# Per-token gate matrices by accumulating scatters in place of TensorE products, with 160 tokens instead of 128 on the gathered path

## The chip, the cores and the metric

One Trainium2 chip, one core. The metric is the device time of one execution in microseconds (us). Five engines work side by side: TensorE (PE, with its weight loads PEld), VectorE (DVE), ScalarE (ACT), GpSimd (POOL) and SyncE (SP), and 16 DMA engines, to which SP, ACT and POOL issue transfers.

## The reference

The kernel is one layer of a decoder on 512 prompt tokens and 8 sample tokens (520 in all, model width 2048, float32). The change touches the second half, a retrieval over 16384 experts, each of which is one row of `u` and one row of `v`:

```python
def peer_route(hn, wq, subkeys):
    q = (hn @ wq).reshape(t, PEER_HEADS, 2, PEER_DKEY // 2)
    s = jnp.einsum('thcd,cnd->thcn', q, subkeys)
    half_s, half_i = lax.top_k(s, PEER_TOPK)
    ...
    experts = (i1 * PEER_NKEYS + i2).reshape(t, -1)
    return experts, jax.nn.softmax(best_s, axis=-1).reshape(t, -1)

def one_chunk(args):
    xc, ec, gc = args
    act = jax.nn.gelu(jnp.einsum('cd,ced->ce', xc, u[ec]))
    return jnp.einsum('ce,ced->cd', gc * act, v[ec])
```

Here `hn` is the normed output of the attention half. Each token picks 8 heads x 16 = 128 expert numbers `ec` with gates `gc`, and its output is the sum over them of gate x gelu(hn . u[e]) x v[e]. An expert number that two heads of a token pick counts twice.

## The kernel before

**Two paths for the tokens.** The first `ND` = 392 tokens are computed densely against all experts: expert tile i is 128 rows of `u`; `u_tile` (line 925) multiplies it by the 392 tokens (16 chunks of the model width, three products each, since each float32 operand is split into a high and a low part: 48 products of 128x392), scales by the norm on DVE (line 930) and applies gelu on ACT. The activation is multiplied by a gate matrix (line 1218; mostly zeros, one number per token and expert), split again (lines 1220 and 1221) into `C`, and multiplied with tile i of `v` in `v_group` (line 1238), which sums over `GRP` = 4 tiles in PSUM and adds the sum to `acc` on DVE (line 1263). The other `NS` = 128 tokens take the gathered path (`gathered`, line 1139): for each of a token's 128 picks POOL gathers 128 rows of 8 KB (one per token, line 1155) from `u`, DVE multiplies and sums them (line 1185); then the same with `v` (line 1197).

**Gate matrices.** After the routing, `build_g` (line 1068) makes, per 4 tokens, one-hot matrices on DVE (lines 1097, 1099), weights them with the gates on ACT and POOL (lines 1101 to 1104), and PE multiplies them (line 1080: 8 products of 128x128), one 128x128 gate matrix per token. ACT copies them to `stg`, and POOL stores 14 pieces to the DRAM tensor `g_d`, from which `load_g` fetches the part of 4 expert tiles.

**Order.** The order of PE and SP is written by hand; POOL's too, from the gathered path on. The other engines are ordered by a scheduler. PE's work is the clock: each 16 products of 260 columns (or as many columns) make one tick (`TICK`), and side work is cut into steps, one of which is emitted per tick. While routing and `build_g` run as such steps, PE computes `u` tiles ahead of their gates: `spill_u` (line 938) stores 70 activations (`NSPILL`) to `act_d`, and `c_of` fetches them later. From `start_experts` (line 1126) on, `v` groups alternate with the `u` tiles that were not spilled, and a gathered row is taken up each `PACE` = 3.1 ticks.

**Weights.** SP loads each weight tile (1 MB) into `wr` (two buffers); ACT rounds it to the high part `wh`, DVE subtracts to the low part `wl`, in halves (lines 297, 299).

**Before the routing.** The `wout` products (line 883) give `acc` for 520 tokens in two products of 260 columns. The operands `HH`, `HG` (high) and `HL`, `HLG` (low) of the dense and the gathered tokens are made from `acc` without the norm; the norm's sum of squares is finished after the first query product (`q_product(0)`, line 911), and the norm multiplies the results (lines 1116, 930).

Of the kernel before, what the change touches and what calls it, by code (L numbers as in the profile page):

```python
# [45 lines left out]
ND, NS = 392, 128  # L46
TT, NTT = 128, 5
TILES = [(ND, NS)] + [(i * (ND // 4), ND // 4) for i in range(4)]
GC, NGC = 28, 14
KA = 12  # L50
NEXP = 128
NSPILL = 70
GRP = 4
TICK = 16
NACT = 3
COPY_EVERY = 9
# [3 lines left out]
NCB = 6  # L60
NGB = 3
PACE = 3.1
PRE = 2
LEAD = 3

C_ID, C_IO, C_N1, C_N2, C_QK, C_SK, C_SR, C_MK, C_END = 0, 128, 256, 272, 288, 292, 300, 301, 317
# [25 lines left out]
def _layout(a):  # L92
# [12 lines left out]
    o["v"] = f["peer_v"][0].reshape(NEXP // GRP, GRP, P, 4, 2, 256).transpose(0, 3, 2, 4, 1, 5)  # L105
# [26 lines left out]
    cst[:64, C_MK:C_MK + 16] = np.arange(64)[:, None] // 4 == np.arange(16)  # L132
    o["cst"] = cst
# [18 lines left out]
def _plan():  # L152
# [10 lines left out]
    p += [("uT", i) for i in range(NSPILL)]  # L163
    for g in range(NEXP // GRP):
        p += [("uT", i) for i in range(g * GRP + (g > 0), min(NEXP, g * GRP + GRP + 1)) if i >= NSPILL]
        p += [("v", (g, q)) for q in range(4)]
# [3 lines left out]
def _program(tc, I, O):  # L170
# [16 lines left out]
    onesR = cp.tile([P, P], F32R, name="onesR")  # L187
    V.tensor_copy(onesR, ones)
# [5 lines left out]
    eg = cp.tile([P, 2, P], F32, name="eg")  # L194
# [3 lines left out]

    def halves(dt):
        a, b = slot("S1a", dt, 8), slot("S1b", dt, 8)  # L200
        return lambda k: (a if k < 8 else b)[:, k % 8]

    def parts(dt):
        a, b = slot("S0", dt, KA), slot("S0g", dt, KC - KA)
        return lambda k: a[:, k] if k < KA else b[:, k - KA]
# [21 lines left out]
    g_d = dp.tile([NGC, P, NK, GC], F32, name="g_d")  # L227


    clock = {"n": 0}  # L230
    first, active, queue = deque(), deque(), deque()

    def soon(f, lag=1):
        first.append((clock["n"] + lag, f))

# [11 lines left out]
    def tick():  # L247
        clock["n"] += 1
        if clock["n"] % COPY_EVERY == 0:
            emit_copy()  # L250
        if first and first[0][0] <= clock["n"]:
            first.popleft()[1]()
        else:
            step()

    def drain(all_=True):
        while first:
            first.popleft()[1]()
        while all_ and (active or queue):
            step()  # L260
# [161 lines left out]
    qk = sp = tab = sbias = qs = kn = vn = None  # L422
# [3 lines left out]
    def start_attention():  # L426
        nonlocal qk, sp, tab, sbias, qs, kn, vn
# [3 lines left out]
        sp = at.enter_context(tc.tile_pool(name="sp", bufs=1))  # L431
        tab = sp.tile([P, 512], F32, name="tab")
# [382 lines left out]
    oa = (lambda k: sl["OA"][:, k], lambda k: sl["OA"][:, 8 + k])  # L815
# [21 lines left out]
    for n in range(2):  # L837
        for c in range(KC):
# [6 lines left out]
            if "sample" in sl and "OA" not in sl and not active and not queue and not first:  # L845
                at.close()
                slp = perm.enter_context(tc.tile_pool(name="sl", bufs=1))
                sl["OA"] = slp.tile([P, KC, T], F32R, name="S2", tag="S2")
# [25 lines left out]
    acc = slp.tile([P, KC, T], F32, name="acc", tag="S2")  # L874
    HHt = slp.tile([P, KC, ND], F32R, name="HH", tag="S3")
    HGt = slp.tile([P, KC, NS], F32R, name="HG", tag="S3g")
    ssq = bt.tile([P, T], F32, name="ssq")
    for c in range(KC):
        w = stream(("wout", c))
        if c < 4:  # L880
            S_.dma_start(acc[:, c * 4:c * 4 + 4, :], I["xT"][:, c * 4:c * 4 + 4, :])
        ps = psum_mm()
        dot3(ps, w, (mH, mL))
        V.tensor_tensor(v2(acc[:, c]), v2(acc[:, c]), ps[:, :, :TH], op=OP.add)
        w2 = cst[:, C_N2 + c:C_N2 + c + 1]
        A.activation(HHt[:, c], acc[:, c, :ND], AF.Copy, scale=w2)
        A.activation(HGt[:, c], acc[:, c, ND:], AF.Copy, scale=w2)
        if c == 0:
            A.activation(ssq, acc[:, c], AF.Square)
        else:  # L890
            s = tmp0()
            A.activation(s, acc[:, c], AF.Square)
            V.tensor_tensor(ssq, ssq, s, op=OP.add)
# [3 lines left out]
    hg = (whole(HGt), whole(HLGt))  # L897
    for c in range(KC):
        w2 = cst[:, C_N2 + c:C_N2 + c + 1]
        V.scalar_tensor_tensor(HLt[:, c], acc[:, c, :ND], w2, HHt[:, c], op0=OP.mult, op1=OP.subtract)  # L900
        V.scalar_tensor_tensor(HLGt[:, c], acc[:, c, ND:], w2, HGt[:, c], op0=OP.mult, op1=OP.subtract)


    def q_product(h):
        w = stream(("wq", h))
        ps = psum_mm()
        terms([(ps[:, 0, :ND], 0, ND), (ps[:, 1, :NS], ND, T)],
              [pick(w, k * P) + tuple((d(k), g(k)) for d, g in zip(hw, hg)) for k in range(KC)])
        return ps

    psq = q_product(0)
    psr = psum_mm()
    rms(ssq, [psr[:, h, :TH] for h in range(2)])
    br.close()
    pr = ExitStack()
    rt = ExitStack()
    ix = rt.enter_context(tc.tile_pool(name="ix", bufs=1))
    tk = ExitStack()
    i1T = ix.tile([P, ND], BF16, name="i1T")
    i2T = ix.tile([P, ND], BF16, name="i2T")  # L920
    gH = ix.tile([P, ND], F32R, name="gH")
    gL = ix.tile([P, ND], F32R, name="gL")
    rstd_ = rstd.rearrange("p h t -> p (h t)")

    def u_tile(i):
# [10 lines left out]
    cell = {}  # L936

    def spill_u():
        nonlocal nu
        act = u_tile(nu)  # L940
        G_.dma_start(act_d[nu], act)
# [384 lines left out]
```

## Time and profile before

| | |
|---|---|
| runs (3) | median 3893.84 us, 3890.56 to 3897.88 |
| profiled execution | 3891.22 us, span from first to last instruction 3889.5 us |
| mean granted TensorE clock | 0.993 of full speed |
| PE busy | 3812.2 us, 98% |
| PEld / DVE / ACT / POOL busy | 97% / 71% / 37% / 24% |
| chain that ended last | PE 84%, DVE 8%, DMA 2% |
| DMA | 901.37 MB, mean 232 GB/s |

Share of busy time is read beside the stage: the table of stretches in the rows below gives it by stage. By the timeline, attention and its projections run to about 1170 us, the output products to 1395, queries and routing to 1832, the gate products to 2180, and the alternation of `u` and `v` tiles to the end, with gathered rows from 2257 to 3750.

### The profile page before, as it was taken

What the parts mean: (1) busy time and instruction counts of PE and PEld (TensorE: products, weight loads), DVE (VectorE), ACT (ScalarE), POOL (GpSimd) and SP (SyncE); (2) the same over time, 40 slices, a digit from 0 to 9 for tenths busy, and PEclk for the clock granted to TensorE, in tenths of its full rate; (3) what the DMA queues carried; (4) which work ended last, traced back from release to release, by engine and by line L of the source; (5) the groups of instructions that cost most, each with busy time, mean ns of one, the idle gap of its engine ahead of it and who ended that gap; (6) DMA issues with size and microseconds to landing.
All of it is one profiled execution on the core that took longest, in us unless ns stands there. A gap on an engine that the chain in (4) does not pass through costs nothing.

```text
span 3889.5 us, 61269 instructions
## 1 busy us (share of the span) xinstructions
PE 3812.2 (98%) x25080; PEld 3779.9 (97%) x25080; DVE 2753.0 (71%) x3925; ACT 1436.4 (37%) x2032; POOL 930.5 (24%) x944
## 2 busy tenths in 40 slices
PE   8999999999999999989999999999999999999999
PEld 8999999999999999989999999999999999999999
DVE  5444333778654357898666579999988888888864
ACT  5655444222322322323777532222222323232232
POOL 2111111223210000133666322222222222222200
PEclk9999999999999999999999999999999999999999
DMA  4233334667656333545544579898888889888853
GB/s 164 103 113 137 141 133 183 222 242 260 228 202 236 141 132 116 191 162 197 199 187 184 201 297 336 319 332 318 333 329 330 318 329 337 331 312 304 331 209 131
DMA packets 140761, 901.37 MB, mean 232 GB/s; under 512 B 20096, under 2 KB 21088, under 8 KB 56512
## 3 DMA queue, kind: packets, MB, share of 16 engines
q1 hardware_dynamic: 59296, 489.74, 33.5%
q0 software_dynamic: 66064, 380.27, 26.4%
q10 hardware_dynamic: 15120, 27.43, 2.2%
q8 instruction: 198, 3.24, 0.3%
q14 instruction: 83, 0.68, 0.1%
HBM read 836.48 MB, written 150.95 MB: 254 GB/s over the span
## 4 chain that ended last, share of the span: by engine, by line
PE 84%; DVE 8%; issue 4%; DMA 2%; ACT 1%; POOL 0%; ACTq 0%; POOLq 0%; DVEq 0%
PE mm L336 71%; PE vv L336 8%; DVE wl L299 3%; PE gq L1080 2%; DVE gb L1185 1%; DMA k<-q_d 1%; PE sc L976 0%; ACT wh L297 0%; DMA wr<-in_win 0%; PE a L510 0%; DVE acc L1263 0%; PE a L517 0%; DVE s1b L1048 0%; PE a L523 0%; DVE c L1221 0%
## 5 line engine op out<-in xcount | busy, mean ns | idle before, releaser
L297 ACT ACTIVATE wh<-wr 128x1024 fp32r<-128x1024 f32 x744 | 787.4, 1059 | 1840.3 <-PE mm L336 1454.3
L299 DVE TENSOR_TENSOR wl<-wr,wh 128x1024 fp32r<-128x1024 f32 x744 | 948.3, 1279 | 335.8 <-ACT wh L297 334.0
L336 PE MATMUL mm<-HH,wl 128*128 128x392 f32 x2176 | 755.1, 347 | 15.3 <-DVE wl L299 15.3
L336 PE MATMUL mm<-HH,wh 128*128 128x392 f32 x2176 | 759.1, 349 | 2.1 <-ACT wh L297 1.2
L336 PE MATMUL mm<-HL,wh 128*128 128x392 f32 x2176 | 756.0, 347 | 0.0
L336 PE MATMUL mm<-c,wh 128*128 128x392 f32 x2316 | 608.5, 343 | 3.9 <-DVE c L1221 3.9
L336 PE MATMUL mm<-S,wh 128*128 128x260 f32 x3048 | 589.0, 285 | 8.2 <-ACT S L380 8.2
L336 PE MATMUL mm<-S,wl 128*128 128x260 f32 x2664 | 545.0, 286 | 5.3 <-DVE wl L299 5.3
L336 PEld LDWEIGHTS mm<-S,wh 128*128 128x128 f32 x3048 | 460.2, 190 | 10.4 <-ACT S L380 8.2
L336 PEld LDWEIGHTS mm<-c,wh 128*128 128x128 f32 x2316 | 426.1, 189 | 6.9 <-DVE c L1221 6.1
L336 PEld LDWEIGHTS mm<-HH,wl 128*128 128x128 f32 x2176 | 412.2, 189 | 19.3 <-DVE wl L299 18.6
L336 PEld LDWEIGHTS mm<-S,wl 128*128 128x128 f32 x2664 | 414.5, 190 | 8.8 <-DVE wl L299 5.7
L336 PEld LDWEIGHTS mm<-HH,wh 128*128 128x128 f32 x2176 | 411.5, 189 | 4.0 <-ACT wh L297 1.5
L336 PEld LDWEIGHTS mm<-HL,wh 128*128 128x128 f32 x2176 | 411.6, 189 | 0.9
L336 PE MATMUL mm<-c,wl 128*128 128x392 f32 x1158 | 396.0, 342 | 1.4 <-DVE wl L299 1.4
L336 PE MATMUL mm<-S1a,wh 128*128 128x260 f32 x1520 | 311.0, 286 | 4.2 <-DVE S1a L381 4.1
L336 PE MATMUL mm<-S1b,wh 128*128 128x260 f32 x1520 | 312.2, 287 | 2.1 <-DVE S1b L381 2.1
L336 PE MATMUL vv<-c,wh 128*128 128x392 f32 x1108 | 293.0, 344 | 8.7 <-DVE c L1221 5.5
L1197 DVE SCALAR_TENSOR_TENSOR hb<-gb,dots,hb 128x2048 f32<-128x2048 f32 x127 | 298.1, 2347 | 4.4 <-DMA gb<-in_vn,idx 4.3
L1185 DVE SCALAR_TENSOR_TENSOR gb<-gb,hb 128x2048 f32<-128x2048 f32 x128 | 292.6, 2286 | 3.1 <-DMA gb<-in_un,idx 3.1
L1155 POOL DMA_INDIRECT gb<-in_vn,idx x128 | 158.7, 1240 | 462.5 <-DVE hb L1197 397.3
L336 PEld LDWEIGHTS mm<-S1a,wh 128*128 128x128 f32 x1520 | 235.0, 189 | 6.2 <-DVE S1a L381 5.1
(317 smaller groups left out, 5584.8 us busy)
## 6 DMA issues: line engine op xcount, KB each, us to landing
wr<-in_uT SPq DMA_DIRECT2D x128, 1024.0 KB, 4.9
wr<-in_v SPq DMA_DIRECT2D x128, 1024.0 KB, 7.3
wr<-in_win SPq DMA_DIRECT2D x78, 1024.0 KB, 4.8
g_d<-stg POOLq DMA_DIRECT2D x14, 1792.0 KB, 6.9
ga<-g_d POOLq DMA_DIRECT2D x32, 784.0 KB, 10.8
wr<-in_wout SPq DMA_DIRECT2D x16, 1024.0 KB, 4.8
out_s<-in_c SPq DMA_DIRECT2D x16, 1020.0 KB, 7.3
act_d<-t POOLq DMA_DIRECT2D x70, 196.0 KB, 2.6
```

The source lines that it names most:

```text
L297: A.activation(h, r, AF.Copy)
L299: V.tensor_tensor(l, r, h, op=OP.subtract)
L336: PE.matmul(ps, u, y[lo >= ND][:, lo % ND:hi - lo + lo % ND] if isinstance(y, tuple) else y[:, lo:hi], start=(begin and i == 0 and a == 0) ...
L1080: PE.matmul(ps[:, t], Bt[:, t], AA[:, t, x], start=x == 0, stop=x == 1)
L1155: G_.indirect_dma_start(out=g, out_offset=None, in_=src, in_offset=bass.IndirectOffsetOnAxis(ap=idx[:, j:j + 1], axis=0))
L1185: V.scalar_tensor_tensor(g, g, 1.0, hn, op0=OP.mult, op1=OP.mult, accum_out=dots[:, j:j + 1])
L1197: V.scalar_tensor_tensor(sums, g, coef[:, j:j + 1], sums, op0=OP.mult, op1=OP.add)
```

## The change

1. 360 tokens are dense, 160 gathered (128 in one pass, 32 in another, whose 128 picks are spread over the 128 partitions as 4 x 32). Products of `u` and `v` tiles have 360 columns. The `wout` products are cut into 360 + 160 columns, the query products too.
2. `build_g` is gone. The gate matrices lie in three DRAM tensors (120 tokens each), which SP fills with zeros during the `wout` products (24 stores); POOL then adds the gates with indirect DMAs that accumulate, one for each of the 128 picks of each third: 384, of up to 120 numbers of 4 bytes. Each waits until the one before it on the same tensor has landed.
3. `v` groups sum over 8 tiles instead of 4; one load is one part of 256 columns for 8 tiles.
4. The norm is multiplied into the operands before they are split, so the multiplication at line 930 goes, and the queries wait for the norm. Two query products run chunk by chunk side by side.
5. The spilled tiles are those not in `INLINE`: the set leaves 101 of 128. In each `v` group the remaining one or two `u` tiles stand among the `C` tiles.
6. Gathered rows start after the first routed tile, one each 6.0 ticks during routing, 3.0 during the scatters, 2.6 afterwards. Cache copies are issued each 7 ticks instead of 9.

```diff
-ND, NS = 392, 128
+ND, NS = 360, 160
+NA_, NB_, RB = 128, 32, 4
...
-GRP = 4
+GRP = 8
+GL = 4
+INLINE = {g * GRP + i for g in range(NEXP // GRP) for i in ((0, 4) if g > 4 else (0,))}
+SPILLED = [i for i in range(NEXP) if i not in INLINE]
+NSPILL = len(SPILLED)
...
-COPY_EVERY = 9
+COPY_EVERY = 7
...
-PACE = 3.1
+PACES = {'routing': 6.0, 'gates': 3.0, 'u': 2.6, 'v': 2.6}
+LEAD = 4
+SCATTER = 0.55
...
+        if cell.get("chains"):
+            cell["chains"]()
+        while posts and posts[0][0] <= clock["n"]:
+            posts.popleft()[1]()
+        if pace and clock["n"] >= pace["due"]:
+            pace["due"] += next(pace["gen"], 1e9)
...
+    def blank(t, i):
+        n = NK * P * GC // 8
+        S_.dma_start(g_d[t][i * n:(i + 1) * n].rearrange("(p x n) o -> p x (n o)", p=P, n=GC * 4),
+                     zero.unsqueeze(1).to_broadcast([P, n // P // (GC * 4), GC * 4]))
...
-        dot3(ps, w, (mH, mL))
...
+        dot3(cut2(ps), w, (mH, mL))
...
+    rms(ssq, [psr[:, h, :TH] for h in range(2)])
...
+            V.scalar_tensor_tensor(x[:, lo:hi], a[:, c], w2, rstd_[:, lo:hi], op0=OP.mult, op1=OP.mult)
+            A.activation(h[:, c], x[:, lo:hi], AF.Copy)
+            V.tensor_tensor(l[:, c], x[:, lo:hi], h[:, c], op=OP.subtract)
...
-        pre = tp.tile([P, ND], F32, name="t0", bufs=2)
-        V.tensor_tensor(pre, ps, rstd_[:, :ND], op=OP.mult)
         act = tp.tile([P, ND], F32, name="t1", bufs=2)
-        A.activation(act, pre, AF.Gelu)
+        A.activation(act, ps, AF.Gelu)
...
+        n, act = nu, u_tile(SPILLED[nu])
+        post(lambda: G_.dma_start(act_d[n], act))
...
-                    PE.matmul(ps[:, t], Bt[:, t], AA[:, t, x], start=x == 0, stop=x == 1)
...
+    def scatter():
+        for c in chains:
+            k, s, due = c
+            if s < P and clock["n"] >= due:
+                G_.indirect_dma_start(out=g_d[k], out_offset=bass.IndirectOffsetOnAxis(ap=at_[k][:GC, s:s + 1], axis=0),
+                                      in_=gt_[k][:GC, s:s + 1], in_offset=None, compute_op=OP.add)
+                c[1:] = s + 1, due + 1 / SCATTER
+        return len(chains) == NGC and all(c[1] == P for c in chains)
...
+    while nu < NSPILL:
+        spill_u()
+        if cell.get("stage") == "gates" and scatter():
+            begin()
```

POOL's order while the gates are made. In the program before, during `build_g` (line 941 stores a spilled activation, 1101 and 1104 weight the one-hot matrices, 1088 stores a piece of the gates):

```order
L941 DMA act_d<-t_22203 128x392
L1101 TENSOR_TENSOR AA<-eA,gH 128x128
L1104 TENSOR_TENSOR AA<-eA,gL 128x4x128
L1088 DMA g_d<-stg 128x3584
L1101 TENSOR_TENSOR AA<-eA,gH 128x128
L1104 TENSOR_TENSOR AA<-eA,gL 128x4x128
L941 DMA act_d<-t_22329 128x392
```

In the changed program, during the scatters (line 1126 a scatter into the tensor named, 1192 a gather of rows, 983 the store of an activation):

```order
L983 DMA act_d<-t_20253 128x360
L1126 DMA g_d_94<-gt_15300,at_15297 1966080x1
L1126 DMA g_d_96<-gt_15302,at_15299 1966080x1
L1126 DMA g_d_95<-gt_15301,at_15298 1966080x1
L1192 DMA rowS3g<-in_un,idx 128x2048
L1126 DMA g_d_94<-gt_15300,at_15297 1966080x1
L1126 DMA g_d_96<-gt_15302,at_15299 1966080x1
L1126 DMA g_d_95<-gt_15301,at_15298 1966080x1
L983 DMA act_d<-t_20326 128x360
```

Between two stores, that is for one `u` tile, stand now six to eight scatters and one or two gathers, where POOL had arithmetic. From the first to the last scatter the order holds 384 scatters, 82 gathers, 65 stores of activations, and six pieces of routing arithmetic.

PE's order where the output products end and the queries begin. Before, the sum of squares (line 364) comes after the 96 products of the first query:

```order
L336 MATMUL mm<-HH,wl 128x392
L336 MATMUL mm<-HG,wl 128x128
L364 MATMUL mm<-ssq,ones 128x260 x2
L336 MATMUL mm<-HH,wh 128x392
L336 MATMUL mm<-HG,wh 128x128
```

In the changed program it stands between the last `wout` product and the first of the queries:

```order
L356 MATMUL mm<-S0g,wl 128x360
L356 MATMUL mm<-S0g,wl 128x160
L384 MATMUL mm<-ssq,ones 128x260 x2
L356 MATMUL mm<-HH,wh 128x360
L356 MATMUL mm<-HG,wh 128x160
L356 MATMUL mm<-HL,wh 128x360
L356 MATMUL mm<-HLG,wh 128x160
```

So every query product is now behind the norm, and each pair of products is 360 + 160 columns wide.

## Rows read from the trace of the kernel before

**Rows 1.** Stretches: busy us of each engine (instructions), clock, DMA share, GB/s.

```profile
1832.00:2180.00 348.00, 348.00 (x2244) 347.96 (x2243) 229.28 (x288) 257.13 (x479) 226.70 (x236) 1.00 0.51 190
2290.00:2900.00 610.00, 587.37 (x3214) 579.41 (x3214) 553.26 (x589) 175.00 (x200) 163.75 (x174) 0.99 0.89 329
3200.00:3300.00 100.00, 100.00 (x561) 99.72 (x560) 89.03 (x72) 30.34 (x36) 26.49 (x20) 1.00 0.91 336
```

**Rows 2.** Chain of waits, in order of time: start us, us, what.

```profile
975.14 411.76 PE mm L336 x3432
...
2927.14 42.94 PE mm L336 x240
```

**Rows 3.** Timeline of PE: start us, us, instruction; query products, then gate products.

```profile
1404.19 0.39 PE L336 MATMUL mm<-HH,wh 128*128 128x392 f32 x1
...
1404.48 0.39 PE L336 MATMUL mm<-HL,wh 128*128 128x392 f32 x1
...
1900.86 1.00 PE L1080 MATMUL gq<-AA,Bt 128*128 128x128 f32 x8
1901.70 0.40 PE L336 MATMUL mm<-HH,wl 128*128 128x392 f32 x1
```

**Rows 4.** Timeline at the norm: PE, DVE and ACT, with [idle before <-releaser].

```profile
1396.00 0.47 PE L336 MATMUL mm<-HLG,wh 128*128 128x128 f32 x1 [5.77 <-DVE HLG L901]
...
1386.92 8.15 DVE L900 SCALAR_TENSOR_TENSOR HL<-acc,cst,HH 128x392 fp32r<-128x392 f32 x15 [0.73 <-PE mm L336]
...
1395.60 4.02 DVE L901 SCALAR_TENSOR_TENSOR HLG<-acc,cst,HG 128x128 fp32r<-128x128 f32 x15
...
1413.16 0.84 ACT L366 ACTIVATE rstd<-mm,epst 128x260 f32<-128x260 f32 x2 [5.76 <-PE mm L364]
1414.02 1.28 ACT L367 ACT_TABLE_LOAD   x1
1415.31 0.64 ACT L367 ACTIVATE rstd<-rstd 128x520 f32<-128x520 f32 x1
```

**Rows 5.** Timeline of POOL at the first gathered rows.

```profile
2260.42 0.93 POOL L1155 DMA_INDIRECT gb<-in_un,idx  x1 [0.30 <-issue]
...
2266.82 1.74 POOL L1232 DMA_DIRECT2D t<-act_d  x3
```

**Rows 6.** DMA issues (KB each, median us to landing); the gathers' least, median, most.

```profile
act_d<-t POOLq DMA_DIRECT2D x70, 196.0 KB, 2.6
t<-act_d POOLq DMA_DIRECT2D x70, 196.0 KB, 7.6
st_d<-st POOLq DMA_DIRECT2D x8, 4.0 KB, 6.9
...
DMA to landing us min/median/max: 5.2/8.0/14.8
```

**Rows 7.** Groups by line: busy us, mean ns, idle before.

```profile
L297 ACT ACTIVATE wh<-wr 128x1024 fp32r<-128x1024 f32 x744 | 787.4, 1059 | 1840.3 <-PE mm L336 1454.3 <-PE vv L336 207.5 <-DMA wr<-in_v 29.2
L299 DVE TENSOR_TENSOR wl<-wr,wh 128x1024 fp32r<-128x1024 f32 x744 | 948.3, 1279 | 335.8 <-ACT wh L297 334.0
L1185 DVE SCALAR_TENSOR_TENSOR gb<-gb,hb 128x2048 f32<-128x2048 f32 x128 | 292.6, 2286 | 3.1 <-DMA gb<-in_un,idx 3.1
L1221 DVE TENSOR_TENSOR c<-t,c 128x392 fp32r<-128x392 f32 x107 | 59.4, 563 | 11.0 <-ACT c L1220 10.6
L1263 DVE TENSOR_TENSOR acc<-acc,mm 128x784 f32<-128x784 f32 x171 | 165.9, 970 | 87.4 <-PE mm L336 86.6
L1045 POOL TENSOR_TENSOR s1a<-s1a,s1b 98x2048 f32<-98x2048 f32 (+1 forms) x10 | 50.3, 5028 | 40.9 <-DVE s1a L1043 40.9
```

**Rows 8.** DMA rate in 40 slices of the stretch 2290 to 2900 us.

```profile
GB/s 385 320 340 369 315 346 241 367 369 317 320 211 365 342 348 359 318 366 284 341 318 352 333 223 362 300 363 360 312 337 332 312 300 358 360 353 297 301 392 266
```

More of the change, by code (lines that the diff above doesn't have):

```diff
@@ L226, in _program @@
     act_d = dp.tile([NSPILL, P, ND], F32, name="act_d")
-    g_d = dp.tile([NGC, P, NK, GC], F32, name="g_d")
+    h_d = dp.tile([P, KC, NS], F32, name="h_d")
+    hn_d = dp.tile([NB_, D], F32, name="hn_d")
+    g_d = [dp.tile([NK * P * GC, 1], F32, name=f"g_d{t}") for t in range(NGC)]
     clock = {"n": 0}
+    cell = {}
+    pace = {}
     first, active, queue = deque(), deque(), deque()
@@ L256, in drain @@
     def drain(all_=True):
[L257 to L260, printed above, removed]
+        while first or posts or all_ and (active or queue):
+            if first or posts:
+                (first or posts).popleft()[1]()
+            else:
+                step()
     copies = []
@@ L431, in start_attention @@
         sp = at.enter_context(tc.tile_pool(name="sp", bufs=1))
+        onesR = sp.tile([P, P], F32R, name="onesR")
+        V.tensor_copy(onesR, ones)
         tab = sp.tile([P, 512], F32, name="tab")
@@ L917, in _program @@
     ix = rt.enter_context(tc.tile_pool(name="ix", bufs=1))
+    at_ = [ix.tile([P, P], I32, name=f"at{t}") for t in range(NGC)]
+    gt_ = [ix.tile([P, P], F32, name=f"gt{t}") for t in range(NGC)]
+    chains = []
     tk = ExitStack()
[L919 to L923, printed above, removed]
     def u_tile(i):
@@ L993, in best_all @@
     def best_all():
[L994 removed]
+        s1a = cp.tile([TT, 3072], F32, name="s1a", tag="S1a")
+        s1x = cp.tile([TT, 1024], F32, name="s1x", tag="S1x")
         bs = k1.tile([TT, PH, TOPK], F32, name="bs")
@@ L1053, in best_all @@
                 V.tensor_copy(eg[:, 1], rows[:, 2])
+                cell["stage"] = "routing"
+                perm.enter_context(tc.manual_schedule(engines={mybir.EngineType.PE, mybir.EngineType.SP, mybir.EngineType.Pool}))
+                pace.update(gen=gathered(), due=clock["n"] + 2)
                 yield
                 continue
-            ps = sc_p.tile([P, 512], F32, name="sc")
-            for x in range(3):
-                PE.transpose(ps[:, x * P:x * P + m], rows[:, x], ident[:m, :m])
@@ L1283, in _program @@
         start_experts()
-    perm.enter_context(tc.manual_schedule(engines={mybir.EngineType.PE, mybir.EngineType.SP, mybir.EngineType.Pool}))
-    queue.append(gathered())
+        load_g(0)
+        load_g(1)
+        cell["stage"] = "experts"
+    while nu < NSPILL:
+        spill_u()
+        if cell.get("stage") == "gates" and scatter():
+            begin()
+    if cell.get("stage") != "experts":
+        drain()
+        while not scatter():
+            clock["n"] += 1
+        begin()
+    drain(False)
     c_of(0)
@@ L1290, in _program @@
         if g == NGRP - 1:
-            cell["rush"] = True
-            drain()
+            for _ in pace["gen"]:
+                pass
         v_group(g)
```

381 lines of the change are left out of this document (182 added, 199 removed).

## The prediction, made before the changed kernel was timed

> **What bounds the kernel now.** I read the page first: PE is busy 98% of the span and carries 84% of the chain that ended last, so a product that goes is time, unless another engine steps in. I then went by stretches [rows 1], because the average hides three regimes. While the gate products are made (1832 to 2180 us) PE is busy without a gap, DVE two thirds of the time and DMA half: only PE matters there. From 2290 to 2900 us, when gathered rows run beside `v` groups of spilled tiles, PE is idle for 610 − 587.4 = 22.6 us, DVE is at 91% and DMA at 0.89: all three are near their end. From 3200 us on PE is full again at a DMA share of 0.91. The chain in order of time gives what a product costs in a long run without waits [rows 2]: 3432 of 260 columns in 411.76 us, 120.0 ns each; 240 of 392 columns in 42.94 us, 178.9 ns each. The slope is 58.9 / 132 = 0.446 ns per column, so a product of 360 columns should take 178.9 − 32 x 0.446 = 164.6 ns.
>
> **PE's part of the change.** The dense products of 392 columns become products of 360: 128 `u` tiles x 48 and 16 `v` groups x 16 x 24, 12288 in all, x 14.3 ns = **−175 us**. The gate products go: by the timeline eight of them hold PE for 0.84 us, from 1900.86 to the next product at 1901.70 [rows 3], and there are 98 such groups: **−82 us**; nothing else waited there [rows 1], so all of it is path.
>
> Against that stand narrow products. In the query products a pair of 392 + 128 columns takes 1404.48 − 1404.19 = 0.29 us [rows 3]: 0.179 for the wide one and 0.11 for the narrow one, where the slope alone would give 0.06. The eight gate products, 128 columns too, took 0.105 each. So a product does not come faster than each 0.11 us, and one of 160 columns (0.075 by the slope) will cost 0.11 as well. The `wout` products, 768 pairs of 260 + 260 at 0.240, become 360 + 160 at 0.165 + 0.11 = 0.275: +26 us. The 384 query pairs go from 0.29 to 0.275: −6. Twenty more transposes at 0.11: +2. Together **+22 us**.
>
> **The norm before the queries.** Now PE waits 5.8 us there for the last low operand [rows 4]. After the change the first query product waits for the addition, the squares and their sum (about 1.6 us at the rows' widths), the norm's own product (some 1.1), then logarithm, table load and exponential on ACT (0.84 + 1.28 + 0.64 [rows 4]). By the order DVE then does eight multiplications before the first subtraction: four of 360 at 0.5 and four of 160 at 0.3 (8.15 / 15 and 4.02 / 15 [rows 4], by width), 3.2 us, and 0.5 for the low operand: near 9.5 us. After that DVE makes a chunk in 4 instructions, 1.6 us, for 6 pairs = 1.65 us on PE; the `wl` halves in between cost a further 3 to 4. So 13 in place of 5.8: **+8 us**; ends 0 and +15.
>
> **POOL in the scatter stage: the open price.** No scatter is in the trace. Its nearest rows are the indirect gather, which POOL begins 0.30 us after the one before and holds for 0.93: 1.23 us a step [rows 5]; and, from below, the plain transfer, three in 1.74, 0.57 a step. I take 1.23, since it is the same instruction with as many indices. From the first to the last scatter POOL's order then holds (384 + 82) x 1.23 + 65 x 0.57 + 4 x 5.0 [rows 7] + some 4 = 634 us, beside 65 `u` tiles of 48 x 164.6 ns = 7.9 us, 514 us. POOL would be the bound, by 120 us. PE is coupled to it: gelu needs one of two buffers that POOL's store frees. The buffers and the six spilled tiles after the last scatter give back about 22, so the floor is some +100. At 0.57 a step it would be 381 us, and nothing.
>
> To that come waits. A scatter waits for the one before it on its tensor. Small stores landed in 2.6 us [rows 6], less than the 3.7 that three scatters take, so alone they would not wait. But a transfer that POOL issues behind a gathered row lands behind it: the reloads of activations took 7.6 us, their stores, before the rows began, 2.6 [rows 6]. So in each of the 82 gather intervals (6.3 us of PE) the fourth scatter waits until the row and the first scatter have landed. At the least landing of a gather, 5.2 [rows 6], plus 0.5, it starts at 5.7; with it, 0.7 of another scatter, the store and arithmetic (1.23 + 0.85 + 0.45 + 0.3) the interval takes 8.53 us: 82 x 2.26 = 185 in all, 163 after the slack. I take the middle of 100 and 163: **+132 us**.
>
> The Trainium skill (DMA: Bandwidth & Descriptors, Anatomy of one DMA) puts a fixed cost of about 2.0 us on each DMA that GpSimd issues and calls transfers under 64 KB mostly overhead, which speaks against 384 transfers of 480 bytes. By that figure a scatter has landed before its successor's turn, and only the floor would stand, an estimate of 3781; the rows have small stores at 2.6, and 6.9 for a store of 4 KB [rows 6], so I go by the rows.
>
> **The alternation of `u` and `v`.** For one weight tile (8.6 us of PE) DVE had in the crowded stretch two `wl` halves, 1.46 rows, two additions of 784 and two `C` steps [rows 7]: 2.56 + 3.34 + 1.94 + 1.13 = 9.0 us by durations that overlap a little. After the change, with 10 tiles for 8 experts (7.9 us each), it has 2.56 + 1.6 x 2.29 + 0.8 x 0.89 + 0.8 x 1.04 = 7.8 us: 0.98 of PE's time against 1.04. So I leave the 22.6 us of waits as they are. DMA grows: 10 tiles and 16 rows of 1.05 MB, and 2.6 MB of activations and gates, 29.8 MB in 79 us, are 378 GB/s (384 in the first five groups, with 9 tiles). The stretch at 0.91 carried 336 [rows 1], which is 369 at a full share; slices of the crowded stretch reached 385 and 392 [rows 8]. Between nothing (392) and 378 / 369 over ten groups and 384 / 369 over five (33 us) I take **+17 us**; what a lower ceiling would make of it is the third rival.
>
> The zero stores (23.6 MB over the 210 us of the `wout` products, +112 GB/s on SP's queue) and the quicker cache copies I cost at nothing: ACT's rounding of the weights waited for PE to free its buffers, 1454 us, and hardly for a load, 29 [rows 7], so loads come early enough to land some us later. If that cover goes, the 16 output products stall, by 1 MB of zeros at 369 GB/s, 3 us a store, at most 70 in all.
>
> **The sum.** The profiled execution took 3891.2 us, 2.6 below the median of the runs. 3891 − 175 − 82 + 22 + 8 + 132 + 17 = **3813 us**. By its own bounds (POOL 100 to 163, norm 0 to 15, DMA 0 to 33) this case lies between 3756 and 3867.
>
> **Rivals.**
> - *POOL keeps pace.* If a scatter costs POOL 0.9 or less (the middle of 0.57 and 1.23 makes 511 us for 514), and the rows' landings overlap, the stage costs nothing: 3681 us. For: 480 bytes are little. Against: the count of indices, not the bytes, is what the two instructions share.
> - *The scatters stand in line behind the rows (slower).* At the median landing of 8.0 [rows 6] the fourth scatter starts at 8.5 and an interval takes 11.33 us: 82 x 5.06 = 415, less 22: 3681 + 393 = 4074 us. It turns the sign from a landing of about 5.8 us on, where the stage costs 210. For: the least is 5.2, close to that. Against: the median is from a stretch with up to three rows under way, at 0.89; here a row comes each 6.3 us.
> - *The memory caps the rate.* If transfers cannot pass 351 GB/s over the alternation, 0.95 of the 369, its ten groups of 79 us stretch by 378 / 351 and five of 71 by 384 / 351, 94 us in place of 17: 3890, no change. For: no stretch of 100 us passed 336 [rows 1]. Against: single slices reached 385 and 392 [rows 8]. The Trainium skill (DMA: Bandwidth & Descriptors, Specifications) names about 358 GB/s as the HBM limit of a core when both cores of its memory read; by that it would be an estimate of 3866, and the two slices contradict it for one core alone.
> - That the change does less than it says I see only in the name: the code spills 101 tiles, not 96. The products are narrower and the gate products are gone in the order.
>
> **Chances.** The forecast 0.45, POOL keeps pace 0.24, the line behind the rows 0.25, the cap 0.06. Runs of this kernel differ by about 0.2%, 8 us, so less than that is "same". Only the second rival, and the crossing into it, lies above 3900; the cap is the "same": faster 0.69, same 0.06, slower 0.25. The range goes from just below the first rival, 3670, up to 3965, a part of the way into the second (landings to 6.7 us); not quite 0.2 is left out, nearly all of it above. Without the slower rival it would be 3670 to 3890.
>
> **What the profile will show.** Long runs of 360 columns at 165 ns; `wout` pairs at 0.275; a wait of some 10 us before the first query product. In the scatter stage: POOL busy without a gap, a scatter each 1.2 us, the fourth after a row waiting for a DMA, and PE idle 1 to 2 us for each `u` tile, released by ACT's gelu or by a late gathered row on DVE. Wrong would be PE full through that stage (first rival), intervals over 9 us between gathers (second), weights late and a DMA share of 0.95 or more in the alternation (third), or PE waiting for `wl` during the output products, which I left at nothing.

## The result, and the profile after

The changed kernel takes **4373.49 us** (median of 4 runs, 4357.27 to 4376.39) against 3892.2 us before (4 runs): ratio 1.1228, 95% interval 1.1196 to 1.126, so 12% slower. 3813 was forecast, with a range up to 3965. The profiled execution took 4376.39 us, its span is 4374.6 us.

The first lines of the profile: busy time of each engine, then tenths of busy time (and of granted clock) in 40 slices of 109 us.

```profile
PE 3758.8 (86%) x24316; PEld 3695.9 (84%) x24316; DVE 2563.3 (59%) x3610; ACT 1250.9 (29%) x1675; POOL 1710.1 (39%) x1329
...
PE   8999999999999999865555555568898999989999
...
POOL 2111111232100002378888888874334343324341
PEclk9999999999999999987777777789999999999999
```

PE's busy time fell from 3812 to 3759 us, and its idle time rose from 77 to 616. A plateau of ten slices has PE at 5 or 6 tenths and POOL at 7 or 8: the scatters. Behind it PE is not full either. The two stretches, with the columns of [rows 1]:

```profile
1856.00:2956.00 1100.00, 649.06 (x3128) 630.94 (x3127) 392.58 (x411) 171.24 (x202) 890.66 (x537) 0.78 0.53 153
3000.00:4200.00 1200.00, 1107.45 (x6432) 1091.60 (x6431) 976.76 (x885) 344.59 (x407) 441.78 (x388) 0.96 0.89 333
```

From the first scatter to the end of the last are **1100 us**, in which PE waits 451; DMA is half idle. In the alternation PE is 92% busy at a clock of 0.96, where [rows 1] had 96%, at 0.99, in 2290 to 2900 us. Its 6432 products there, at 0.1646 us, are 1059 us of work: 141 of 1200 us are lost, 93 as idle time and the rest in products that take longer beside the lower clock.

Who waits for whom between 1856 and 2956 us (total us, times, longest), first PE, then ACT:

```profile
PE mm L356 <- ACT t L975: 450.8, 60, 15.2
...
ACT t L975 <- DMA act_d<-t: 500.6, 64, 14.4
```

PE waits for gelu, gelu for a buffer, and the buffer for the store that stands in POOL's queue among scatters: 7.5 us for each of 60 `u` tiles. The scatters by themselves (least, median and most of their durations in ns, then time to landing; the last line is the gathers' landing in the same stretch):

```profile
L1126 POOL DMA_INDIRECT g_d<-gt,at x384: 1582/1628/3737, 1856.4 to 2954.7; - x192
...
DMA to landing us min/median/max: 2.9/4.2/8.7
...
DMA to landing us min/median/max: 5.3/5.7/8.6
```

A scatter holds POOL for 1.6 us, where the gather of [rows 5] held it for 0.93. With the 0.30 before it that is a step of 1.9, not 1.23. POOL's timeline shows the step, and one scatter of 3.25 us:

```profile
2103.48 1.01 POOL L1192 DMA_INDIRECT rowS3g<-in_un,idx  x1 [0.30 <-DVE wl L319]
2104.79 1.67 POOL L1126 DMA_INDIRECT g_d<-gt,at  x1 [0.30 <-issue]
2106.76 1.60 POOL L1126 DMA_INDIRECT g_d<-gt,at  x1 [0.30 <-issue]
2108.66 1.59 POOL L1126 DMA_INDIRECT g_d<-gt,at  x1 [0.30 <-issue]
2111.16 3.25 POOL L1126 DMA_INDIRECT g_d<-gt,at  x1 [0.91 <-DMA g_d<-gt,at]
2114.71 1.59 POOL L1126 DMA_INDIRECT g_d<-gt,at  x1 [0.30 <-issue]
```

The long one runs beside this instruction on DVE, and ends 1.47 us after it:

```profile
2110.65 2.29 DVE L1210 SCALAR_TENSOR_TENSOR rowS3g<-rowS3g,hb 128x2048 f32<-128x2048 f32 x1 [7.32 <-DMA rowS3g<-in_un,idx]
```

Counted over the trace, 110 of the 384 scatters took 1.75 us or more, and every one overlaps a DVE instruction: by the longest overlap 58 that of a gathered row, 49 a `wl` half, 3 routing arithmetic. Of the other 274, 190 overlap none, and those took 1.68 at most; 84 overlap one and are no longer for it. What all 384 took above 1.6 us adds up to 123 us.

The scatter after a gather does wait for a landing (0.91 above), but not for long. POOL's waits for scatters' landings in 1840 to 1990, 1990 to 2850 and 2850 to 2960 us:

```profile
POOL g_d L1126 <- DMA g_d<-gt,at: 20.2, 12, 4.2
...
POOL g_d L1126 <- DMA g_d<-gt,at: 28.9, 28, 2.5
...
POOL g_d L1126 <- DMA g_d<-gt,at: 26.4, 13, 5.0
```

In the 860 us in which all three tensors take turns the waits are 29 us. The other 47 lie at the two ends, where scatters of one or two tensors follow each other.

The small terms can be read at the norm (PE's timeline, with idle time before an instruction):

```profile
1425.13 0.44 PE L356 MATMUL mm<-S0g,wh 128*128 128x360 f32 x2
1425.41 0.44 PE L356 MATMUL mm<-S1y,wh 128*128 128x360 f32 x2
...
1428.91 1.14 PE L384 MATMUL mm<-ssq,ones 128*128 128x260 f32 x4 [2.79 <-DVE ssq L930]
1434.10 0.67 PE L356 MATMUL mm<-HH,wh 128*128 128x360 f32 x1 [4.04 <-ACT HH L943]
1434.57 0.34 PE L356 MATMUL mm<-HG,wh 128*128 128x160 f32 x1
1436.71 0.67 PE L356 MATMUL mm<-HL,wh 128*128 128x360 f32 x1 [1.80 <-DVE HL L944]
...
1437.30 0.58 PE L356 MATMUL mm<-HH,wl 128*128 128x360 f32 x1
...
1437.82 0.58 PE L356 MATMUL mm<-HH,wh 128*128 128x360 f32 x1
```

A `wout` pair takes 0.28 us (0.275 forecast). PE waits 2.79 + 4.04 + 1.80 = 8.6 us at the norm in place of 5.8 [rows 4]. Behind that wait pairs begin 0.52 us apart, about twice 0.275: the granted clock is 0.50 there (1436 to 1440 us), the lower of its two levels, 1.2 of 2.4 GHz, after PE stood idle. And a long run of 360-column products, from the chain (start us, us, what), takes 31.73 / 192 = 0.1653 us each, for 0.1646 forecast:

```profile
3489.27 31.73 PE mm L356 x192
```

### The profile page after: what moved, and what is told of

It is laid out like the page before. It is cut to its first block, busy times and chain, and to the rows that moved or that the text cites. A ratio compares the mean times of both kernels' runs of the same rounds, so it can differ in the third digit from the quotient of the medians.

```text
span 4374.6 us, 59233 instructions
## 1 busy us (share of the span) xinstructions
PE 3758.8 (86%) x24316; PEld 3695.9 (84%) x24316; DVE 2563.3 (59%) x3610; ACT 1250.9 (29%) x1675; POOL 1710.1 (39%) x1329
## 4 chain that ended last, share of the span: by engine, by line
PE 53%; POOL 15%; issue 12%; DMA 10%; DVE 8%; ACT 1%; ACTq 0%; POOLq 0%; DVEq 0%; SPq 0%
PE mm L356 44%; POOL g_d L1126 11%; PE vv L356 6%; DMA g_d<-gt,at 4%; DVE wl L319 3%; DVE hb L1221 1%; DMA wr<-in_v 1%; POOL rowS2g L1192 1%; POOL rowS3g L1192 1%; POOL rowS0g L1192 1%; POOL act_d L983 1%; ACT wh L317 1%; DMA rowS2g<-in_un,idx 1%; DMA rowS3g<-in_vn,idx 1%; DMA rowS0g<-in_vn,idx 1%
## 5 line engine op out<-in xcount | busy, mean ns | idle before, releaser
L356 PE MATMUL mm<-HH,wh 128*128 128x360 f32 x2176 | 786.8, 362 | 459.9 <-ACT t L975 455.1
L1126 POOL DMA_INDIRECT g_d<-gt,at x384 | 737.8, 1921 | 187.9 <-issue 100.0
L356 PE MATMUL mm<-HH,wl 128*128 128x360 f32 x2176 | 770.3, 354 | 17.3 <-DVE wl L319 17.3
L356 PE MATMUL mm<-HL,wh 128*128 128x360 f32 x2176 | 770.9, 354 | 1.8 <-DVE HL L944 1.8
L356 PE MATMUL mm<-S,wh 128*128 128x260 f32 (+2 forms) x2698 | 540.7, 289 | 8.0 <-ACT S L400 8.0
L356 PE MATMUL mm<-S,wl 128*128 128x260 f32 (+2 forms) x2474 | 513.8, 289 | 3.6 <-DVE wl L319 3.6
L356 PE MATMUL mm<-c8S1b,wh 128*128 128x360 f32 x1120 | 282.4, 333 | 8.6 <-ACT c8S1b L1252 6.4
L356 PE MATMUL mm<-cb,wh 128*128 128x360 f32 x1072 | 269.5, 332 | 2.5 <-ACT cb L1252 1.3
L356 PE MATMUL mm<-S1b,wh 128*128 128x260 f32 (+1 forms) x1140 | 238.8, 291 | 0.9 <-DVE S1b L401 0.9
L356 PE MATMUL mm<-S1a,wh 128*128 128x260 f32 (+1 forms) x1140 | 238.9, 291 | 0.7 <-DVE S1a L401 0.6
```

The source lines that it names most:

```text
L356: PE.matmul(ps, u, y[lo >= ND][:, lo % ND:hi - lo + lo % ND] if isinstance(y, tuple) else y[:, lo:hi], start=(begin and i == 0 and a == 0) ...
L1126: G_.indirect_dma_start(out=g_d[k], out_offset=bass.IndirectOffsetOnAxis(ap=at_[k][:GC, s:s + 1], axis=0), in_=gt_[k][:GC, s:s + 1], in_of ...
```

## The experiments

The theory after this reading, **A**: POOL's work in the scatter stage (the price of a scatter, held up by DVE) is most of the loss, and the transfers' rate in the alternation the rest. Rivals: landings behind gathered rows; DVE's own work; the other parts of the change; a third cost. All of these kernels start from the changed one. Each ran once, unless an interval is given; the four runs of the changed kernel lie within 20 us of each other.

**Without scatters.** The order and the paces stay.

```diff
-                G_.indirect_dma_start(out=g_d[k], out_offset=bass.IndirectOffsetOnAxis(ap=at_[k][:GC, s:s + 1], axis=0),
-                                      in_=gt_[k][:GC, s:s + 1], in_offset=None, compute_op=OP.add)
...
-    V.memset(zero, 0.0)
+    V.memset(zero, 0.01)
```

> The changed kernel without its 384 scatters; order and paces are otherwise the same. It leaves out the gates: the gate tensors hold a constant 0.01 instead. In the changed kernel the stage from the first scatter to the last took 1098 us (1856 to 2955) with PE 57% busy. Theory A (POOL's scatters set that stage): without them it runs at PE's pace, 65 tiles of 7.9 us = 514 us and some more, so 4373 - 1098 + 514 to 560 = 3790 to 3835 us, while the alternation after it keeps its waits (PE 92% busy). Rival (the rows gathered in that stage, or the lower clock, set it): PE stays below 80% there and the time above 4150.

Measured: 4985 us, with a granted clock of 0.65 over the whole execution, from the first slice on, long before anything that differs. This says nothing about scatters, and the kernel was run once more:

> The kernel without scatters once more (gates left out, the gate tensors hold 0.01). Theory A: the stage between the routing and the alternation runs at PE's pace and the time is 3790 to 3835 us; from there on PE stays about 92% busy, as in the changed kernel. Rival: PE below 80% in that stage, over 4150 us.

Measured: **3812.96 us**. Two stretches, first from the first place of a scatter to the last spilled tile, then 1200 us of the alternation:

```profile
1856.00:2424.00 568.00, 550.96 (x3308) 548.85 (x3307) 417.67 (x449) 176.62 (x214) 215.83 (x172) 0.99 0.86 322
2430.00:3630.00 1200.00, 1108.28 (x6437) 1092.33 (x6436) 976.21 (x884) 344.73 (x407) 431.39 (x387) 0.96 0.89 333
```

PE is 97% busy in the stage; the same gathers and stores run beside it. So the scatters cost 4373 − 3813 = 560 us, and the alternation's loss is independent of them: the second row is almost the one of the changed kernel. That this run's time is the forecast's 3813 is chance: the forecast had 132 for the scatters and 17 for the transfers.

**Waits for landings.** Every second scatter goes to a tensor of its own.

```diff
-                G_.indirect_dma_start(out=g_d[k], out_offset=bass.IndirectOffsetOnAxis(ap=at_[k][:GC, s:s + 1], axis=0),
+                G_.indirect_dma_start(out=(g_x if s % 2 else g_d)[k], out_offset=bass.IndirectOffsetOnAxis(ap=at_[k][:GC, s:s + 1], axis=0),
```

> Every second scatter of a third goes to another tensor that nobody reads (half of the gates are left out of the result), so a scatter waits for the one six before it instead of three; POOL issues as many instructions as before. Theory A (the price of an instruction on POOL): 384 x (1.62 + 0.30) + 83 gathers x (1.02 + 0.30) + 65 stores x 0.65 + 20 = about 910 us for the stage in place of 1098, and 4373 - 190 = about 4185 us. Rival, the line behind the rows (a landing that is waited for is most of the loss): the stage falls below 750 us and the time below 4030. If waits for landings do nothing, 4373 stays.

Measured: 4291.44 us, 82 less, and a stage of 1023 us. POOL's waits for scatters' landings fell from 75.5 to 9.1 us, and that is most of what was won. What scatters took above 1.6 us I had called a wait too, and it stayed, at 95 of 123 us: it is no wait for a landing, so 910 was too low. The line behind the rows as the main cause is out.

**Prices of a scatter.** The first third of the tokens as it is, the second without the addition, the last with half of its indices.

```diff
+                if k == 0:
...
+                elif k == 1:
+                    G_.indirect_dma_start(out=g_d[k], out_offset=bass.IndirectOffsetOnAxis(ap=at_[k][:GC, s:s + 1], axis=0),
+                                          in_=gt_[k][:GC, s:s + 1], in_offset=None)
+                else:
+                    G_.indirect_dma_start(out=g_d[k], out_offset=bass.IndirectOffsetOnAxis(ap=at_[k][:GC // 2, s:s + 1], axis=0),
+                                          in_=gt_[k][:GC // 2, s:s + 1], in_offset=None, compute_op=OP.add)
```

> Prices of one scatter on POOL, each third of the tokens on a line of its own: the first third as it is (120 numbers, added), the second third as plain stores without the addition, the last third with 60 of its 120 numbers (gates counted twice and half of a third are left out of the result). The full scatter took 1.62 us. If the addition costs, the plain third takes about 1.0 as the gathers do and the half third still 1.3 to 1.6; if the count of indices costs, the plain third takes 1.6 and the half third about 0.9. Either way some 128 x 0.6 to 0.7 = 80 to 90 us less: about 4290 us.

Measured: 4317.79 us. Least, median and most of the durations in ns, by line:

```profile
L1127 POOL DMA_INDIRECT g_d<-gt,at x128: 1581/1652/3519, 1853.9 to 2778.8; - x128
...
L1130 POOL DMA_INDIRECT g_d<-gt,at x128: 998/1025/3085, 1917.0 to 2851.4; - x128
...
L1133 POOL DMA_INDIRECT g_d<-gt,at x128: 1428/1451/3246, 1980.8 to 2910.5; - x128
```

The addition costs 0.6 us of POOL; half the indices save only 0.2. If the price grows evenly with the indices, 0.2 / 60 = 0.0033 us each, 120 of them are an estimated 0.4 us of the 1.65, and most of a scatter is a fixed price. Plain, it takes what a gather does. The time fell by 56 us, not 80 to 90: by the medians the two cheaper thirds save 128 x 0.63 + 128 x 0.2 = 106 us, but scatters beside DVE took back some of it (all 384 together 658 us for 738), and waits for landings rose from 75 to 115.

**Rows out of the scatter stage.**

```diff
-        if pace and clock["n"] >= pace["due"]:
+        if pace and cell["stage"] != "gates" and clock["n"] >= pace["due"]:
...
         cell["stage"] = "experts"
+        pace["due"] = clock["n"] + 1
```

> No gathered row is taken up while the gates are scattered; the rows go on after the last scatter, at the same pace as in the changed kernel. If landings behind rows make the waits of the scatters, POOL's 83 gathers (110 us) and nearly all of the 190 us of waits go: the stage takes about 800 us in place of 1098, still bound by POOL (theory A), with PE near 65%. If the scatters wait for each other's own landings, the waits stay and the stage takes 950 to 990. The rows come back later: 231 + 83 rows at some 5.3 us are 1660 us after the stage in place of 1420, so 4310 us in the first case, about 4480 in the second.

Measured: 4397.04 us, a stage of 891 us. The 210 us that it lost are neither of the two sums expected: 61 of 75 us of landing waits are still there, so they are not the rows' doing. What went are the gathers themselves, 76 of 82 (six come before the edit takes hold), 76 x 1.39 = 106 us, and 92 of the 123 us by which scatters were longer than 1.6. The time is 24 us longer all the same, because the rows now come last and PE waits 250 us for them:

```profile
PE gt L1231 <- DVE hb L1221: 249.9, 2, 226.4
```

With the gathers both their transfers and DVE's multiplications had left the stage. Since every long scatter had run beside a DVE instruction, the suspect became DVE.

**DVE beside the scatters.** The same gathers, but a short multiplication.

```diff
-                V.scalar_tensor_tensor(g, g, 1.0, hn, op0=OP.mult, op1=OP.mult, accum_out=dots[:, j:j + 1])
+                n = D if cell["stage"] == "experts" else 512
+                V.scalar_tensor_tensor(g[:, :n], g[:, :n], 1.0, hn[:, :n], op0=OP.mult, op1=OP.mult, accum_out=dots[:, j:j + 1])
```

> The changed kernel, but while the gates are scattered DVE multiplies only 512 of the 2048 columns of a gathered row (0.6 instead of 2.3 us; that part of the gathered tokens' sums is left out); all transfers and waits stay. In the changed kernel 110 of the 384 scatters took 1.75 us or more, 119 us above 1.6 in all, and each of them ran beside a DVE instruction, 56 of them beside a row's multiplication. Theory (POOL cannot go on with a scatter while such a DVE instruction runs): what is over 1.6 falls to 45 to 60 us, the stage from 1100 to some 1030, the time to 4300 to 4315. Rival (the gathers' transfers make scatters long): the stage stays at 1080 to 1100 and the time above 4350.

Measured: 4277.32 us, a stage of 1024 us; above 1.6 us are 43 us in place of 123.

```profile
L1126 POOL DMA_INDIRECT g_d<-gt,at x384: 1577/1617/3171, 1845.7 to 2867.5; - x192
...
  DMA g_d<-gt,at: 88.6, 56
```

The stage is 76 us shorter with every transfer in place, and landing waits even rose to 88.6. So the rows' multiplications did hold POOL up. (The time fell by 96 us, where 4300 to 4315 us was expected; the 20 us outside the stage are not explained.) The `wl` halves seem to hold it too: 57 of the 67 long scatters that are left lie beside one, and in the changed kernel 33 of the 68 scatters that overlap `wl` halves alone are long, by up to 1.0 us. No run made these halves shorter.

**The alternation: transfers or DVE?** First 1 KB in place of 8 KB for a row, with DVE about as busy; then whole rows, with a quarter of DVE's work.

```diff
-                    G_.indirect_dma_start(out=g, out_offset=None, in_=src,
+                    thin = cell["stage"] == "experts"
+                    G_.indirect_dma_start(out=g[:, :256] if thin else g, out_offset=None,
+                                          in_=src.rearrange("e (x n) -> (e x) n", x=8) if thin else src,
```

> In the alternation each gathered row is fetched as 1 KB instead of 8 KB (the sums read this piece over and over, 7/8 of the columns in the u pass, so DVE works nearly as long; the gathered tokens' result is left wrong by that). The alternation of the changed kernel (3000 to 4200 us) had PE 92% busy at a clock of 0.96: 1200 us for 6432 products of 0.1646 = 1059 us, 141 us lost, with a DMA share of 0.89 and 333 GB/s. If the transfers' rate is the cause, PE is over 98% busy there and the time falls by 110 to 150 us, to about 4225 to 4265. If DVE's work is, nothing changes: over 4340.

```diff
-                V.scalar_tensor_tensor(g, g, 1.0, hn, op0=OP.mult, op1=OP.mult, accum_out=dots[:, j:j + 1])
+                n = 512 if cell["stage"] == "experts" else D
+                V.scalar_tensor_tensor(g[:, :n], g[:, :n], 1.0, hn[:, :n], op0=OP.mult, op1=OP.mult, accum_out=dots[:, j:j + 1])
...
-                    V.scalar_tensor_tensor(sums, g, dots[:, j:j + 1], sums, op0=OP.mult, op1=OP.add)
+                    V.scalar_tensor_tensor(sums[:, :512], g[:, :512], dots[:, j:j + 1], sums[:, :512], op0=OP.mult, op1=OP.add)
```

> In the alternation DVE multiplies and sums only 512 of the 2048 columns of each gathered row (0.6 instead of 2.3 us a row, most of the gathered tokens' sums left out); the rows are fetched whole. If DVE's work is what PE waits for in the alternation, PE is over 98% busy and the time about 4225 to 4265; if the transfers' rate is, a DMA share of 0.89 or more stays and the time above 4330.

Measured: thin rows 4274.05 us (−99; 4225 to 4265 was expected), narrow sums 4355.60 (−18, just below the least of the changed kernel's four runs). The alternation of the two, columns as above:

```profile
3000.00:4100.00 1100.00, 1069.04 (x6376) 1063.85 (x6377) 954.46 (x873) 338.80 (x399) 467.36 (x387) 0.99 0.55 188
```

```profile
3000.00:4200.00 1200.00, 1129.02 (x6590) 1115.91 (x6590) 673.81 (x908) 353.73 (x423) 387.92 (x406) 0.97 0.90 342
```

With thin rows DVE is 87% busy, more than before, and PE 97%, in whole stretches 100%. With narrow sums DVE falls to 56% and PE stays at 94%, with the transfers at 0.90. So it is the rows' transfers. They reach PE in part by way of late weights: in the changed kernel, from 2990 us on, the rounding of the weights on ACT waits for loads (total us, times, longest), 140 us in all. With thin rows it is 8 us, and in the kernel before, from 2290 us on, 34.

```profile
ACT wh L317 <- DMA wr<-in_v: 114.4, 44, 4.9
...
ACT wh L317 <- DMA wr<-in_uT: 25.3, 11, 5.7
```

Whether the rate alone does it, or also that loads of activations and gates stand behind rows in POOL's queue, these runs don't separate: thin rows take both away.

**Both costs away**, the kernel without scatters with thin rows:

> The changed kernel without its scatters and with 1 KB in place of 8 KB for each gathered row in the alternation (gates left out, the gathered tokens' result left wrong). If the two costs found so far are all, they add up: 4373 - 560 (as without the scatters alone) - 99 (as with the thin rows alone) = 3714 us, near the 3681 + 8 that the products and the norm alone gave. If a third cost is left in the alternation (DVE's work, or the wait for activations and gates), the time stays above 3760.

Measured: 3697.66 us, for 3714 expected. The costs add up to within 16 us, and no third cost of their size is left.

**Gate products back.** `build_g` of the kernel before, in place of zero stores and scatters; the rest of the change stays.

```diff
-GC, NGC = ND // 3, 3
+GC, NGC = 24, 15
...
-            chains.append([k, 0, clock["n"] + 1.0])
+        queue.append(build_g())
```

> The gate matrices made by PE as in the kernel before (15 pieces of 24 tokens), without zero stores and scatters; all else as in the changed kernel: 160 gathered tokens, sums over 8 tiles, the norm in the operands, the paces. Theory A: no stage is bound by POOL. PE's products are 3681 + 90 x 0.84 = 3757 us; with 10 to 13% lost over the some 1500 us in which rows run beside the tiles, 3890 to 3950. Rival: if the other parts of the change (not the scatters) had cost the time, it stays above 4200.

Measured: 3994.24 us, 379 less than the changed kernel, so the other parts of the change did not cost the time; but it is 44 above the range expected and still 100 above the kernel before. The stage in which the gates are made, and a stretch of the alternation:

```profile
1940.00:2350.00 410.00, 356.20 (x2158) 345.74 (x2159) 314.54 (x324) 272.01 (x450) 316.93 (x268) 0.93 0.68 251
2600.00:3800.00 1200.00, 1100.63 (x6373) 1084.82 (x6372) 968.63 (x874) 342.55 (x406) 402.64 (x333) 0.95 0.89 331
```

The alternation loses the same 8%, and the gate products now lose 13%, 45 us of it waiting for POOL's share of the one-hot matrices, which stands among gathers. Two versions of this kernel try other paces of the rows (5.0 ticks while the gates are made, and then also 3.0 in place of 2.6 afterwards):

```diff
-PACES = {'routing': 6.0, 'gates': 3.0, 'u': 2.6, 'v': 2.6}
+PACES = {'routing': 6.0, "gates": 5.0, 'u': 2.6, 'v': 2.6}
```

> As e7 (gates by PE products), but a gathered row only each 5.0 ticks instead of 3.0 while the gates are made. In e7 that stage took 406 us with PE 87% busy: 45 us of waits for POOL's part of the one-hot matrices, and a lower clock. With fewer gathers and row multiplications it should take about 330 us with PE over 95% busy; 240 rows are then left for the alternation: 457 MB at 335 GB/s = 1365 us, from about 2425 on: 3790 us and a tail, 3800 to 3850 in all, 1 to 2% faster than the kernel before. Rival (what is gained in the stage comes back in the alternation, since the rows move there): 3920 to 3990.

> As e9, with a row each 3.0 ticks instead of 2.6 once the gates are made. If the transfers' rate binds the alternation, slower rows only move its bytes: PE waits less beside the rows, but they end later, and the time is within 1% of e9's. If PE's waits there were bursts of rows that a slower pace avoids, the time is 1 to 2% below e9's.

Measured: 3959.47 us (ratio to before 1.0162, 1.0145 to 1.0179) and 4025.32 (1.0335, 1.0314 to 1.0357). In the first, 3800 to 3850 was missed and the rival's 3920 to 3990 came out: the stage shrank to 370 us, but its rows came back, and 34 us of the end are a wait for the last of them. In the second neither sum came out: it lies 1.7% above the first, where within 1% or below was expected. The longer wait of the second, PE at the end of the gathered path:

```profile
PE gt L1257 <- DVE hb L1247: 147.6, 1, 147.6
```

Slower rows let PE run better beside them (its busy time is 1156 of 1200 us from 2600 to 3800, in the first version 1136) and then keep it waiting 148 us for those that are left. With 320 rows the time that PE gains by narrower products is taken back by the rows, at either pace: in waits beside them or in a wait for the last.

**Fewer rows.** The first of these two kernels with 384 dense and 136 gathered tokens, so 272 rows, one each 3.2 ticks (10.0 while the gates are made); `wout` products of 260 + 260 again.

```diff
-ND, NS = 360, 160
-NA_, NB_, RB = 128, 32, 4
+ND, NS = 384, 136
+NA_, NB_, RB = 128, 8, 16
...
-GC, NGC = 24, 15
+GC, NGC = 24, 16
...
-PACES = {'routing': 6.0, "gates": 5.0, 'u': 2.6, 'v': 2.6}
+PACES = {'routing': 6.0, 'gates': 10.0, 'u': 3.2, 'v': 3.2}
```

> A version between the two: gates by PE products as in the kernel before, 384 dense and 136 gathered tokens, 272 rows in place of 320, a row each 3.2 ticks (10 while the gates are made), the output products cut 260 + 260 again; sums over 8 tiles and the norm in the operands stay. PE's products: 3891 - 12288 x 8 x 0.446 ns = 44 + 13 for the norm = 3860 us; the alternation needs 161 to 171 GB/s for rows and some 167 for tiles, activations and gates, 330 to 338, which the transfers can give. So 3830 to 3890, 0 to 2% faster than before. If 340 GB/s is not to be had beside everything else, or the rows end late, over 3900.

Measured: 3947.08 us (1.0131, 1.0107 to 1.0156), 57 above the range expected. The alternation is as hoped:

```profile
2600.00:3800.00 1200.00, 1175.18 (x6697) 1170.67 (x6696) 960.96 (x868) 357.08 (x415) 382.23 (x318) 0.99 0.86 320
```

PE is 98% busy at 320 GB/s. The gain goes elsewhere, for the most part: PE waits 30 us for DVE in the routing, beside the first rows, 16 in the gate stage and 18 for the last rows. No version run here beats the kernel before.

## Why the prediction was wrong

The direction was wrong, and the time lies above the range. By the runs the way from 3891 to 4373 us is:

| term | forecast | shown |
|---|---|---|
| dense products, gate products | −175, −82 | 0.1653 us a product for 0.1646; the gate products are gone |
| narrow products | +22 | a `wout` pair 0.28 for 0.275 |
| norm | +8 | 8.6 us of waits for 5.8, and some us at the lower clock |
| scatter stage | +132 | **+560** (without scatters 3813) |
| transfers in the alternation | +17 | **+115** (3813 − 3698) |
| the rest | 0 | 3698 − (3891 − 175 − 82 + 22 + 8 = 3664) = +34 |

**The step that failed** is the price of a scatter: "I take 1.23, since it is the same instruction with as many indices". Its step, where DVE does not lengthen it, is 1.60 + 0.30 = 1.90 us, since the addition alone costs POOL 0.6: 384 x 0.67 = 257 us more. Of the way from POOL's floor, forecast at 634 us, to the stage of 1100 this is more than half. The bounds were one-sided: both ends, 0.57 and 1.23, came from instructions that do less than a scatter, and nothing bounded it from above.

**The second part was not foreseen at all**: DVE holds POOL up, 123 us by the durations, of which shorter row multiplications took away 80. The evidence stood in the trace before, in the line of the gathers (least, median and most of the durations, in ns), where I had taken one gather from the timeline:

```profile
L1155 POOL DMA_INDIRECT gb<-in_un,idx x128: 932/940/2832, 2257.8 to 3017.3; - x128
```

Of the 256 gathers of that kernel 70 took over 1.1 us, and all 70 overlap a DVE instruction; the most is three times the median. The Trainium skill (SBUF — State Buffer, SBUF: two separate sides) says that DVE and GpSimd share a pair of ports, that it is an exclusive lock and not a sharing of bandwidth, and that GpSimd cannot write the descriptors of its DMAs while DVE runs an instruction in a 2-port mode; of DVE instructions with two inputs in SBUF it says that they take the lock only against GpSimd instructions that read SBUF. The traces agree that DVE can hold up a DMA that GpSimd issues: the scatter at 2111.16 us grows by 1.65 beside a DVE instruction of 2.29 us. Here both the row's multiplication and the `wl` half have two inputs in SBUF. That the ports are the mechanism no run here shows; they show the delay.

**The waits were mis-told.** I argued that the fourth scatter after each row would wait 2.26 us for the row's landing, 185 us in all. The rows' landing was as assumed (5.7 us for 5.2), but the waits in the middle of the stage are 29 us. At 1.9 us a step the next scatter of the same tensor comes due 5.7 us after the last anyway, mostly behind the landing, median 4.2. The same slow price that broke the floor made the waits vanish. With the sum put right, 730 us for 384 scatters at 1.90, 123 beside DVE, 75 of landing waits, 114 of gathers, some 42 of stores and 24 of arithmetic, POOL needs 1108 us; the stage took 1100.

**The slower rival** had the time's side and the sign of the profile, over 9 us between gathers (74 from 1912 to 2890 us: 13 us each), but a wrong cause: its landings are not what made them late.

**The transfers.** The term's form was right, its size too small: +17 was taken between nothing and 33, by a rate of 369 GB/s at a full share. A stretch of 1200 us gives 333 at 0.89, hardly more than the kernel before (329 at 0.89 [rows 1]), so the third rival's cap was nearer: it gave 94 us, and 99 to 115 were measured. Of its signs late weights came, a share of 0.95 or more did not, so a cap on the rate is not shown. Single slices and rate times share were the wrong rows to trust; the sustained rate was in [rows 1] and needed no scaling. In the version with gate products 100 us of `u` tiles did carry more:

```profile
2400.00:2500.00 100.00, 100.00 (x607) 100.00 (x606) 73.34 (x65) 31.70 (x38) 37.73 (x33) 1.00 0.93 364
```

The Trainium skill (DMA: Bandwidth & Descriptors, Specifications) gives about 358 GB/s as the limit of a core, half of what its memory has for two. This row of one core passes it, and the alternation, at 333, stays below it, so that figure is not the bound here.

**What was left at nothing** and held: the zero stores and cache copies cost PE no wait that the runs show. What did not is spread over the kernel. Of the remaining 34 us 9 are the products (12288 x 0.7 ns). The others are idle time of PE, 110 us in the run of 3698 for 77 before, of which 8 had been forecast for the norm. Of these 33 us more, 15 lie beside the spilled tiles (11 in a single wait for gelu), 8 in the alternation and 8 ahead of the first scatter's place. Routing has no part in it: between the norm and the first scatter PE is idle for 18 us in the changed kernel, and between the norm and the gate products for 17.5 before.

## What to carry to other kernels

A new instruction's price is bounded from above only by something that does at least as much: an indirect DMA that adds is not a gather of the same count, and a few of them measured first would have decided this change. When work moves to a queue, count every instruction on it, at its step and not its busy time, and ask which engine can hold it up while it runs. And when two engines and the transfers are all near their end, taking columns from PE by adding rows to gather is paid in bytes at the sustained rate of the trace.

## What the hardware showed that was not expected

- An indirect DMA of 120 numbers of 4 bytes holds POOL for 1.63 us in the median when it accumulates, 1.03 when it only stores; with 60 numbers and the addition 1.45.
- A DVE instruction with two operands in SBUF (a `wl` half of 1.2 us, a row of 2.3 us) can lengthen the scatter that runs beside it, by up to 2.1 us; with the row's instruction cut to 0.6 us, what scatters took above 1.6 us fell from 123 to 43 us over the stage.
- 120 accumulated numbers landed after 4.2 us in the median and 2.9 at the least, so a chain in which each waits for the landing of the one before went no faster than one each 2.9 us here.
